# The opening of a three-stage transformer block in one written order, with later loads behind it

## The chip, the cores and the metric

The kernel runs on one core of a Trainium2 chip. The metric is the device time of one execution in microseconds (us). The times of the kernel before are of three runs: 1593.21, 1597.02 and 1598.21 us, median 1597.02 us.

In the profile the engines are PE (TensorE, the matrix products; PEld are its weight loads), DVE (VectorE), ACT (ScalarE), POOL (GpSimd) and SP (SyncE, which here only issues loads). ACT issues some loads too; both engines issue in the order of their own instructions.

## The reference

Two streams of 256 tokens and 1024 features (the latent x and a context) go through two layers. Each layer is a swiglu, a mixer and a second swiglu; the first layer's mixer is a short convolution, the second's is attention. Before each of these stands a normalisation with a modulation whose vectors come from a product with a large matrix:

```
mod  = (silu(c) @ mod_w[i] + mod_b[i])            # 9 vectors of 1024 for the latent
modc = (silu(c_ctx) @ mod_w[i] + mod_b[i])        # and 9 for the context
h    = rms(x, norm_g) * (1 + scale) + shift       # shift, scale: two of the nine
x    = x + 0.5 * gate * ((silu(h @ w13_gate) * (h @ w13_up)) @ w2)
```

The hidden size of a swiglu is 2816, 22 tiles of 128.

## The kernel before

Features lie on the 128 partitions (8 blocks k of 128), tokens on the free axis: 256 latent columns and 256 context columns, 512 together. Every fp32 operand is split into an upper part (`hi`, cast by ACT in `split`, line 98) and a lower part (`lo`, subtracted by DVE, line 99). A product is then three matmuls: upper weights by upper data, upper weights by lower data, lower weights by upper data (`mm3`, lines 122 to 124).

The first swiglu's first three tiles (0, 1, 2) are made in an opening of their own, because their input h needs the modulation's first two vectors (shift `B00`, scale `A00`), which are made on PE, one quarter q (two blocks k) at a time. The opening is a string of steps, `FIRST_STEPS`, taken in order:

- `Pcq` (`mod_pe`): loads a quarter of channel c (1 is scale, 0 is shift; two loads of 512 KB into `pm`), multiplies it by the silu of c on PE (line 757), and copies the row off with ACT.
- `Tcq` (`mod_turn`): turns the row to columns on PE (line 769); DVE adds the bias (line 774).
- `Nq` (`norm_q`): DVE scales x (line 264), ACT adds the shift and casts (`hh`, line 274), DVE subtracts (`hl`, line 275), for two blocks and two streams.
- `F` (`fill`): idle matmuls on a matrix of ones, `FILL` of them.
- `Wi` (`first_w`): loads tile i's weights (1 MB) and splits them.
- `Miq` (`first_mm`): tile i's products for quarter q, 12 matmuls of 512 columns.
- `Hq` (`copy_q`): ACT keeps an fp32 copy of h for the block sums.
- `S` (`load_sc`): loads c for all partitions (`scbc`) and takes its silu.

Only PE keeps this order (`manual_schedule` with PE alone). DVE, ACT and SP are ordered by a scheduler that works from modelled times and lets later work slip in where it thinks an engine is free; a DMA's semaphore is also taken up again only when an earlier load has landed.

After the opening come the gate products of the three tiles (`w13_post`), the block sums of h (`FirstBlocks.sums`: eight sums of 512 columns on DVE, lines 376 to 383, each kept split by ACT and DVE as `th`, `tl`), which serve the block products of later tiles, and six units of modulation (`tick(6)`). A unit (`mod_unit`, line 142) is one DVE reduction of 1024 columns that makes part of a later modulation vector out of a loaded piece of `modT` (1 MB for two or four units) and `scbc`. `tick(n)` adds n to a debt and pays it in whole units. Then `ffn` makes tiles 3 to 7 in the plain way (`tick(5)` after each), projects eight tiles with `w2` (`project`, `tick(ev)` after most of its eight outputs), and goes on with two more thirds of seven tiles and a projection each. `mod_ready` pays at once for what a consumer needs and isn't made yet.

Buffers that matter: three raw weight tiles (`wr`), four split halves (`wh`, `wl`), eight pairs of `gh`, `gl` (which hold tile 2's split weights, the copies H and the gate products in turn), and 16 tiles `hop` (h, the loaded rows, later the block sums).

Of the kernel before, what the change touches and what calls it, by code (L numbers as in the profile page):

```python
# [16 lines left out]
P = 128  # L17
D = 1024
KT = D // P
# [7 lines left out]
KVH = 2  # L27
EPS = 1e-6
WARM = 36
FILL = 8  # L30

FIRST_STEPS = (
    "P10 P00 T10 T00 N0 F W0 M00 W1 P11 P01 T11 T01 N1 H0 M10 W2 M01 P12 H1 M11 P02 T12 T02 "
    "N2 M20 H2 M21 P13 P03 T13 T03 N3 M02 M12 M22 H3 M03 M13 M23 S"
)


# [1 line left out]
def hybrid_kernel(ctx: ExitStack, tc: tile.TileContext, a: dict, out: bass.AP):  # L42
# [53 lines left out]

    def split(hi, lo, src):
        nc.scalar.activation(out=hi, in_=src, func=AF.Copy)  # L98
        nc.vector.tensor_tensor(out=lo, in0=src, in1=hi.bitcast(F32), op=ALU.subtract)  # L99

    def half():

# [515 lines left out]
    def ffn(l, b, h, tot, gate, tail, gs=(), ev=1.5):  # L618
        gs = list(gs)
        i0 = 0  # L620
        for t, n in enumerate(THIRDS):
            between = ()
            if tot == T2:
                heads = []
                if t == 0 and not gs:

                    w = [load_w(a["w13"][l, b, 0])]
                    gs = [new_pair("g") for _ in range(2)]
                    pp = [(psum("pg"), psum("pu")) for _ in range(2)]
                    w13_mm(pp[0], w[0], h, range(KT), 0, S)  # L630
                    flush()
                    w.append(load_w(a["w13"][l, b, 1]))
                    w13_mm(pp[1], w[1], h, range(KT), 0, S)
                    h.sums(0)
                    w13_mm(pp[0], w[0], h, range(KT), S, T2)
                    w13_post(pp[0], gs[0], 0, T2)
                    heads.append(Pair(a["w13"][l, b, 2], h))
                    h.sums(1)
                    heads[0].sums(0)
                    w13_mm(pp[1], w[1], h, range(KT), S, T2)  # L640
                    w13_post(pp[1], gs[1], 0, T2)
                    heads[0].head()
                    h.sums(2)
                    heads[0].sums(1)
                prev = None
                for i in range(len(gs), n):
                    if t == 0 and not heads and i in AS_IS[l, b]:
                        w = load_w(a["w13"][l, b, i])
                        pp = psum("pg"), psum("pu")
                        if prev:  # L650
                            prev.seven()
                        w13_mm(pp, w, h, range(4), 0, T2)
                        if prev:
                            gs.append(new_pair("g"))
                            prev.four(gs[-1])
                            prev = None
                        w13_mm(pp, w, h, range(4, KT), 0, T2)
                        gs.append(new_pair("g"))
                        w13_post(pp, gs[-1], 0, T2)
                        tick(5)  # L660
                        continue
                    if heads:
                        pr = heads.pop(0)
                    else:
                        pr = Pair(a["w13"][l, b, i0 + i], h)
                        pr.sums(0)
                        pr.sums(1)
                        pr.head()
                    pr.five()
                    if prev:  # L670
                        prev.seven()
                    pr.six()
                    if prev:
                        gs.append(new_pair("g"))
                        prev.four(gs[-1])
                    prev = pr

                def last():
                    gs.append(new_pair("g"))
                    prev.four(gs[-1])  # L680

                between = (prev.seven, last) if prev else ()
            else:
                for i in range(n):
                    w = load_w(a["w13"][l, b, i0 + i])
                    gs.append(new_pair("g"))
                    pp = psum("pg"), psum("pu")
                    w13_mm(pp, w, h, range(KT), 0, tot)
                    w13_post(pp, gs[i], 0, tot)
                    tick(1)  # L690
            i0 += n
            box = {}

            def ws2(m):
                if m // 2 not in box:
                    src = a["w2a"][l, b, m // 2] if t == 0 else a["w2b"][l, b, t - 1, m // 2]
                    box[m // 2] = load_raw(src, 2 * n * P)
                raw = box[m // 2]
                o = (m % 2) * n * P
                hi, lo = half()  # L700
                split(hi[:, : n * P], lo[:, : n * P], raw[:, o : o + n * P])
                return lambda k: (hi[:, k * P : k * P + P], lo[:, k * P : k * P + P])

            cur = gs
            end = t == len(THIRDS) - 1
            project(
                ws2, lambda k, c0, c1: (cur[k][0][:, c0:c1], cur[k][1][:, c0:c1]), n,
                gate, tail if end else None, tot, 2 if end and tot == T2 else 0, ev, between,
            )
            gs = []  # L710
# [32 lines left out]

    rows = {}

    def mod_pe(ch, q):


        raws = []
        for i in range(2):  # L750
            raws.append(hot("pm", F32))
            nc.sync.dma_start(raws[i], a["mod0"][ch, q, :, i * 1024 : i * 1024 + 1024])
        pr = psum("pr") if (ch, q) == (1, 0) else psmall("pr")
        for k in range(KT):
            g = 32 * (k % 4)
            o = k % 4 * S
            nc.tensor.matmul(
                pr[g : g + 32, :S], sccol[:, k, :], raws[k // 4][:, o : o + S],
                start=(k < 4), stop=(k >= 4), tile_position=(0, g),
            )  # L760
        row = tp.tile([P, T2], F32, name=nm("row"), tag="gm", bufs=3)
        nc.scalar.copy(row[:, :S], pr[:, :S])
        rows[ch, q] = pr, row
# [14 lines left out]
            op=ALU.add,  # L778
        )

    def norm_q(q):
        k2 = slice(2 * q, 2 * q + 2)
        nc.vector.tensor_tensor(
            out=A00[:, k2, :], in0=A00[:, k2, :], in1=both(normg[:, 0, 0, k2]), op=ALU.mult
        )
        for k in range(2 * q, 2 * q + 2):
            for s in range(2):
                t = None
                if k % 2:
                    t = tp.tile([P, T2], F32, name=nm("t"), tag="sg", bufs=3)[:, :S]  # L790
                ts[k, s] = norm_k(s, k, h, A00, B00, ris[s], t)

    def copy_q(q):
        for s in range(2):
# [10 lines left out]
    def first_mm(i, q):  # L805
        if q == 0:
            pps[i] = psum("pg"), psum("pu")
        w13_mm(pps[i], ws[i], h, range(2 * q, 2 * q + 2), 0, T2)

    ws, gs0 = {}, []  # L810

    def load_sc():
        for v in range(2):
            nc.sync.dma_start(scbc[:, v, :], a["c2"][v : v + 1, :].to_broadcast([P, D]))
            nc.scalar.activation(out=scbc[:, v, :], in_=scbc[:, v, :], func=AF.Silu)

    def first_w(i):
        if i < 2:
            ws[i] = load_w(a["w13"][0, 0, i], fine=True)
            return  # L820
        raw = load_raw(a["w13"][0, 0, i])
        parts = [new_pair("w") for _ in range(4)]
        for j in (0, 2, 1, 3):
            split(*parts[j], raw[:, j * T2 : j * T2 + T2])
        ws[i] = lambda o: tuple(t[:, o % T2 : o % T2 + P] for t in parts[o // T2])

    steps = {
        "P": mod_pe,
# [1 line left out]
        "F": lambda: fill(FILL),  # L830
        "H": copy_q,
        "S": load_sc,
        "W": first_w,
        "N": norm_q,
        "M": first_mm,
    }
    with tc.manual_schedule(engines={mybir.EngineType.PE}):
        fill(WARM)
        sums = [rms_sum(s, (accs[s], accs[s, "last"])) for s in range(2)]
        for step in FIRST_STEPS.split():  # L840
            if step == "P00":
                for s in range(2):
                    ris.append(tp.tile([P, S], F32, name=nm("ris"), tag=f"ris{s}", bufs=1))
                    nc.scalar.copy(ris[s], rms_all(*sums[s]))
            steps[step[0]](*(int(c) for c in step[1:]))
    done[0, 0] = done[0, 1] = 16
    h = FirstBlocks(h, h32)
    for i in range(3):
        gs0.append(new_pair("g"))
        w13_post(pps[i], gs0[i], 0, T2)  # L850
    h.sums()
    tick(6)

    convk = cload("convk", [P, 3, KT])
    qg = cload("qg", [P, 1])
    kg = cload("kg", [P, 1])
    cosT = cload("cosT", [P, S])
    sinT = cload("sinT", [P, S])


    hn = Plain()
    ffn(0, 0, h, T2, lazy_gate(0, 0), tail_norm(0, 1, hn), gs0, 1.8)
    h = hn

    zs = []
# [359 lines left out]
```

## Time and profile before

| what | value |
|---|---|
| median of three runs | 1597.02 us |
| profiled execution | 1595.53 us, its span 1593.7 us |
| mean granted PE clock in the span | 0.993 |
| PE busy | 1568.8 us, 98% |
| DVE busy | 1303.3 us, 82% |
| ACT busy | 721.1 us, 45% |
| moved by DMA | 248.79 MB, mean 156 GB/s |

A line of the timeline is: start, length, engine, line of the code, operation, output, inputs, count, and in brackets how long the engine had been idle and what ended that. A line of a window is: the window, its length, then busy time and count of each engine asked for, the granted PE clock (1.00 is full), the DMA share and GB/s. Matmuls are pipelined and overlap in the records, so the pace is the distance of their starts.

### The profile page before, as it was taken

Reading aid. Unit: us, or ns where it says so; the run is one execution under the profiler, and the core shown is the slowest. Engines: PE = TensorE matmul, PEld = TensorE weight load, DVE = VectorE, ACT = ScalarE, POOL = GpSimd, SP = SyncE. Lnnn points to the kernel's source line nnn. Section 1 sums busy time; section 2 is a strip of 40 time slices with the busy share of each in tenths; the row PEclk is TensorE's granted clock in tenths of the full one; section 3 lists DMA queues with packets and bytes.
Section 4 is the critical chain, followed back from the end, with each engine's and each line's share of the span. In section 5 each row is a group of like instructions: output and inputs, shape, how many; then the busy total and the mean of one; then the engine's idle time right before and its main releaser. Section 6 shows DMA issues by size and latency. Waiting matters only on the chain.

```text
span 1593.7 us, 25820 instructions
## 1 busy us (share of the span) xinstructions
PE 1568.8 (98%) x10666; PEld 1449.7 (91%) x10666; DVE 1303.3 (82%) x1984; ACT 721.1 (45%) x1103; POOL 29.4 (2%) x20
## 2 busy tenths in 40 slices
PE   8999999999999999999999999999999998899999
PEld 7688998999888899989899899899899897899999
DVE  5998888979999879798798879898797789876554
ACT  6522452544322356335345365335255455644443
POOL 0000000000000000000000000000000005200000
PEclk9999999999999999999999999999999999999999
DMA  9465324334565522452342513443433554556452
GB/s 359 181 238 207 110 99 153 133 102 176 177 219 195 175 68 93 148 170 100 129 156 96 180 56 107 158 136 99 169 118 120 208 186 151 200 185 220 166 200 102
DMA packets 39575, 248.79 MB, mean 156 GB/s; under 512 B 5409, under 2 KB 7201, under 8 KB 14625
## 3 DMA queue, kind: packets, MB, share of 16 engines
q1 hardware_dynamic: 36864, 245.38, 43.9%
q10 hardware_dynamic: 2592, 1.76, 0.4%
q8 instruction: 83, 1.36, 0.3%
q14 instruction: 36, 0.29, 0.1%
HBM read 244.77 MB, written 1.05 MB: 154 GB/s over the span
## 4 chain that ended last, share of the span: by engine, by line
PE 92%; DVE 4%; ACT 2%; DMA 1%; issue 0%; POOL 0%; ACTq 0%; DVEq 0%; POOLq 0%
PE py L123 10%; PE py L122 10%; PE py L124 10%; PE p L124 7%; PE p L123 7%; PE p L122 6%; PE q L122 5%; PE q L124 5%; PE q L123 5%; PE pg L122 2%; PE pg L124 2%; PE pg L123 2%; PE pu L124 2%; PE pu L123 2%; PE pu L122 2%; PE pv L122 1%
## 5 line engine op out<-in xcount | busy, mean ns | idle before, releaser
L98 ACT ACTIVATE wh<-wr 128x1024 fp32r<-128x1024 f32 (+2 forms) x276 | 276.4, 1014 | 388.0 <-PE py L123 140.7
L99 DVE TENSOR_TENSOR wl<-wr,wh 128x1024 fp32r<-128x1024 f32 (+2 forms) x276 | 319.9, 1166 | 88.2 <-ACT wh L98 87.9
L142 DVE CUSTOM_DVE_ANT_0 junk<-wr,scbc,modb 128x1024 bf16<-128x1024 f32 x224 | 286.9, 1281 | 31.8 <-DMA wr<-in_modT 29.0
L122 PE MATMUL py<-gh,wh 128*128 128x512 f32 (+1 forms) x746 | 263.3, 353 | 0.0
L123 PE MATMUL py<-gl,wh 128*128 128x512 f32 (+1 forms) x746 | 263.0, 353 | 0.0
L124 PE MATMUL py<-gh,wl 128*128 128x512 f32 (+1 forms) x746 | 262.7, 352 | 0.0
L99 DVE TENSOR_TENSOR wl<-ws,wh 128x1024 fp32r<-128x1024 f32 x108 | 131.6, 1223 | 34.1 <-ACT wh L98 34.0
L124 PEld LDWEIGHTS py<-gh,wl 128*128 128x128 f32 x746 | 141.1, 189 | 19.0
L122 PEld LDWEIGHTS py<-gh,wh 128*128 128x128 f32 x746 | 141.2, 189 | 18.6
L123 PEld LDWEIGHTS py<-gl,wh 128*128 128x128 f32 x746 | 141.2, 189 | 18.1
L98 ACT ACTIVATE wh<-ws 128x1024 fp32r<-128x1024 f32 x108 | 113.9, 1058 | 71.3 <-PE p L123 44.5
L124 PE MATMUL p<-th,wl 128*128 128x256 f32 x432 | 122.3, 283 | 0.0
L123 PE MATMUL p<-tl,wh 128*128 128x256 f32 x432 | 122.2, 283 | 0.0
L122 PE MATMUL p<-th,wh 128*128 128x256 f32 x432 | 122.2, 283 | 0.0
L453 DVE SCALAR_TENSOR_TENSOR x<-py,G,x 128x256 f32<-128x256 f32 x168 | 73.9, 477 | 23.1 <-PE py L124 23.1
L122 PE MATMUL q<-bh,wh 128*128 128x256 f32 x320 | 90.6, 283 | 0.0
L123 PE MATMUL q<-bl,wh 128*128 128x256 f32 x320 | 90.6, 283 | 0.0
L124 PE MATMUL q<-bh,wl 128*128 128x256 f32 x320 | 90.6, 283 | 0.0
L122 PEld LDWEIGHTS p<-th,wh 128*128 128x128 f32 x432 | 82.9, 192 | 0.3
L123 PEld LDWEIGHTS p<-tl,wh 128*128 128x128 f32 x432 | 82.9, 192 | 0.3
L124 PEld LDWEIGHTS p<-th,wl 128*128 128x128 f32 x432 | 82.9, 192 | 0.0
L124 PE MATMUL pg<-hh,wl 128*128 128x256 f32 (+1 forms) x240 | 75.5, 315 | 2.8 <-DVE wl L99 2.7
(236 smaller groups left out, 4045.2 us busy)
## 6 DMA issues: line engine op xcount, KB each, us to landing
wr<-in_w SPq DMA_DIRECT2D x88, 1024.0 KB, 4.9
wr<-in_modT SPq DMA_DIRECT2D x64, 1024.0 KB, 5.0
wr<-in_w2b SPq DMA_DIRECT2D x32, 896.0 KB, 4.6
wr<-in_w2a SPq DMA_DIRECT2D x16, 1024.0 KB, 4.9
pm<-in_mod SPq DMA_DIRECT2D x16, 512.0 KB, 10.0
wr<-in_cw_cx SPq DMA_DIRECT2D x8, 1024.0 KB, 4.9
wr<-in_cw_b SPq DMA_DIRECT2D x4, 1024.0 KB, 5.0
wr<-in_cw_out SPq DMA_DIRECT2D x4, 1024.0 KB, 4.9
```

Of the source, the lines that this page charges most:

```text
L98: nc.scalar.activation(out=hi, in_=src, func=AF.Copy)
L99: nc.vector.tensor_tensor(out=lo, in0=src, in1=hi.bitcast(F32), op=ALU.subtract)
L122: nc.tensor.matmul(ps, wh, mh, start=first, stop=False, **kw)
L123: nc.tensor.matmul(ps, wh, ml, start=False, stop=False, **kw)
L124: nc.tensor.matmul(ps, wl, mh, start=False, stop=last, **kw)
L142: nc.vector.tensor_tensor_reduce(out=junk, in0=raw[:, j * D : j * D + D], in1=scbc[:, v, :], scale=1.0, scalar=modb[:, l, col : col + 1], ...
L453: nc.vector.scalar_tensor_tensor(out=x[:, m, s * S : s * S + S], in0=ps[:, o : o + S], scalar=g[:, m, s : s + 1], in1=x[:, m, s * S : s * ...
```

## The change

The opening's string becomes an order for four queues: PE, DVE, ACT and SP all keep it. For this the steps are cut finer:

- `Lcq` loads the rows that `Pcq` uses, `Ri` a tile's raw weights. `Wip` splits one quarter of them, in the order pair 2, 0, 3, 1.
- `Uq` scales x with A (it needs no shift); `Nqj` adds the shift, casts and subtracts for one block.
- M00 and M10 come ahead of P11 and P01; in them the order of the products changes, and M10 takes those with lower weights last.
- `FILL` is 4 in place of 8.
- `S` stays last, now on ACT and SP too. The five constants of later stages (convk, qg, kg, cosT, sinT) are issued on ACT's queue behind the last silu of `S`.
- The block sums are traced in `ffn` behind tile 3's weight load, and their DVE instructions are put behind the last subtract of tile 1's weights.
- `tick(6)` goes, one unit is taken off the debt ahead of tile 3, and `ev` of the first swiglu goes from 1.8 to 2.1.

```diff
-FILL = 8
+FILL = 4
 FIRST_STEPS = (
-    "P10 P00 T10 T00 N0 F W0 M00 W1 P11 P01 T11 T01 N1 H0 M10 W2 M01 P12 H1 M11 P02 T12 T02 "
-    "N2 M20 H2 M21 P13 P03 T13 T03 N3 M02 M12 M22 H3 M03 M13 M23 S"
+    "L10 L00 R0 R1 P10 T10 U0 P00 L11 L01 T00 F N00 W00 W01 N01 W02 W03 M00 R2 W10 W11 W12 "
+    "W13 H0 M10 P11 L12 P01 L02 T11 U1 T01 N10 N11 M01 W20 W21 H1 M11 W22 W23 P12 L13 P02 L03 "
+    "T12 U2 T02 M20 N20 N21 H2 M21 P13 P03 T13 U3 T03 M02 N30 N31 M12 M22 M03 H3 M13 M23 S"
 )
...
+                        if "T1" not in h.t:
+                            with tc.issue_after(rows["W1"]):
+                                h.sums()
+                            owed[0] -= 1
                         w13_mm(pp, w, h, range(4), 0, T2)
...
+    def mod_load(ch, q):
+        rows[ch, q] = [hot("pm", F32) for _ in range(2)]
+        for i in range(2):
+            nc.sync.dma_start(rows[ch, q][i], a["mod0"][ch, q, :, i * 1024 : i * 1024 + 1024])
...
+    def norm_one(q, j):
+        k = 2 * q + j
+        for s in range(2):
+            hh = pick(h, k, s * S, s * S + S)[0]
+            nc.scalar.activation(
+                out=hh, in_=ts[k, s], func=AF.Identity, bias=B00[:, k, s : s + 1]
+            )
+        for s in range(2):
+            hh, hl = pick(h, k, s * S, s * S + S)
+            nc.vector.scalar_tensor_tensor(
+                out=hl, in0=ts[k, s], scalar=B00[:, k, s : s + 1], in1=hh.bitcast(F32),
+                op0=ALU.add, op1=ALU.subtract,
+            )
...
+        if i < 2 and q == 0:
+            order = [(k, n, lo) for k in range(2) for lo in range(3) for n in range(2)]
+            if i:
+                order.sort(key=lambda o: (o[2] == 2, o[1] if o[2] == 2 else 0))
+            for k, n, lo in order:
+                nc.tensor.matmul(
+                    pps[i][n], ws[i]((1 - n) * 1024 + k * P)[lo == 2],
+                    pick(h, k, 0, T2)[lo == 1], start=k == 0 and lo == 0, stop=False,
+                )
+            return
...
+    def first_w(i, p):
+        j = (2, 0, 3, 1)[p]
+        ins = split(*cut[i][j], raws[i][:, j * T2 : j * T2 + T2])
+        rows[f"W{i}"] = ins.ins
...
-    with tc.manual_schedule(engines={mybir.EngineType.PE}):
+    queues = [nc.tensor, nc.vector, nc.scalar, nc.sync]
+    with tc.manual_schedule(engines={e.engine for e in queues}):
...
-    h.sums()
-    tick(6)
-
-    convk = cload("convk", [P, 3, KT])
...
+    with tc.issue_after(rows["last"]):
+        convk = cload("convk", [P, 3, KT])
+        qg = cload("qg", [P, 1])
...
-    ffn(0, 0, h, T2, lazy_gate(0, 0), tail_norm(0, 1, hn), gs0, 1.8)
+    ffn(0, 0, h, T2, lazy_gate(0, 0), tail_norm(0, 1, hn), gs0, 2.1)
```

More of the change, by code (lines that the diff above doesn't have):

```diff
@@ L98, in split @@
         nc.scalar.activation(out=hi, in_=src, func=AF.Copy)
-        nc.vector.tensor_tensor(out=lo, in0=src, in1=hi.bitcast(F32), op=ALU.subtract)
+        return nc.vector.tensor_tensor(out=lo, in0=src, in1=hi.bitcast(F32), op=ALU.subtract)
     def half():
@@ L744, in hybrid_kernel @@
     rows = {}
+    def mod_load(ch, q):
+        rows[ch, q] = [hot("pm", F32) for _ in range(2)]
+        for i in range(2):
+            nc.sync.dma_start(rows[ch, q][i], a["mod0"][ch, q, :, i * 1024 : i * 1024 + 1024])
     def mod_pe(ch, q):
[L749 to L752, printed above, removed]
+        raws = rows[ch, q]
         pr = psum("pr") if (ch, q) == (1, 0) else psmall("pr")
@@ L779, in mod_turn, with scale_q @@
         )
-    def norm_q(q):
+    def scale_q(q):
         k2 = slice(2 * q, 2 * q + 2)
@@ L790, in norm_q @@
                     t = tp.tile([P, T2], F32, name=nm("t"), tag="sg", bufs=3)[:, :S]
-                ts[k, s] = norm_k(s, k, h, A00, B00, ris[s], t)
+                ts[k, s] = scaled(s, k, A00, ris[s], t)
+    def norm_one(q, j):
[11 more added lines that the diff above has]
+            )
     def copy_q(q):
@@ L807, in first_mm @@
             pps[i] = psum("pg"), psum("pu")
+        if i < 2 and q == 0:
[8 more added lines that the diff above has]
+            return
         w13_mm(pps[i], ws[i], h, range(2 * q, 2 * q + 2), 0, T2)
-    ws, gs0 = {}, []
+    ws, gs0, raws, cut = {}, [], {}, {}
     def load_sc():
@@ L814, in load_sc, with first_raw @@
             nc.sync.dma_start(scbc[:, v, :], a["c2"][v : v + 1, :].to_broadcast([P, D]))
-            nc.scalar.activation(out=scbc[:, v, :], in_=scbc[:, v, :], func=AF.Silu)
-    def first_w(i):
+            last = nc.scalar.activation(out=scbc[:, v, :], in_=scbc[:, v, :], func=AF.Silu)
+        rows["last"] = last.ins
+    def first_raw(i):
+        raws[i] = load_raw(a["w13"][0, 0, i])
         if i < 2:
[L819 to L825, printed above, removed]
+            ts_ = [half() for _ in range(2)]
+            cut[i] = [tuple(t[:, c : c + T2] for t in ts_[j]) for j in range(2) for c in (0, T2)]
+        else:
+            cut[i] = [new_pair("w") for _ in range(4)]
+        ws[i] = lambda o: tuple(t[:, o % T2 : o % T2 + P] for t in cut[i][o // T2])
+    def first_w(i, p):
+        j = (2, 0, 3, 1)[p]
+        ins = split(*cut[i][j], raws[i][:, j * T2 : j * T2 + T2])
+        rows[f"W{i}"] = ins.ins
     steps = {
@@ L832, in hybrid_kernel @@
         "S": load_sc,
+        "L": mod_load,
+        "R": first_raw,
         "W": first_w,
-        "N": norm_q,
+        "U": scale_q,
+        "N": norm_one,
         "M": first_mm,
     }
-    with tc.manual_schedule(engines={mybir.EngineType.PE}):
+    queues = [nc.tensor, nc.vector, nc.scalar, nc.sync]
+    with tc.manual_schedule(engines={e.engine for e in queues}):
         fill(WARM)
@@ L840, in hybrid_kernel @@
         for step in FIRST_STEPS.split():
-            if step == "P00":
+            if step == "U0":
                 for s in range(2):
@@ L850, in hybrid_kernel @@
         w13_post(pps[i], gs0[i], 0, T2)
-    h.sums()
-    tick(6)
-    convk = cload("convk", [P, 3, KT])
[L855 to L858, printed above, removed]
+    with tc.issue_after(rows["last"]):
+        convk = cload("convk", [P, 3, KT])
+        qg = cload("qg", [P, 1])
+        kg = cload("kg", [P, 1])
+        cosT = cload("cosT", [P, S])
+        sinT = cload("sinT", [P, S])
     hn = Plain()
-    ffn(0, 0, h, T2, lazy_gate(0, 0), tail_norm(0, 1, hn), gs0, 1.8)
+    ffn(0, 0, h, T2, lazy_gate(0, 0), tail_norm(0, 1, hn), gs0, 2.1)
     h = hn
```

## The prediction

> **What bounds the kernel now.** I read the page's first table, then a table of windows over the first 128 us, then the chain of waits and the timeline there.
>
> ```profile
> span 1593.7 us, 25820 instructions
> PE 1568.8 (98%) x10666; PEld 1449.7 (91%) x10666; DVE 1303.3 (82%) x1984; ACT 721.1 (45%) x1103; POOL 29.4 (2%) x20
> ```
>
> TensorE (PE) is busy for 98% of the span, so only what shortens PE's time, or removes its waits, can pay. Nothing in the diff takes away a product that the result needs. What PE has to lose therefore lies in the 24.9 us in which it is not busy and in time that is busy but slow or useless. Windows (columns: PE busy and its matmuls, granted clock, DMA share, GB/s):
>
> ```profile
> 0.00:11.60 11.60, 10.57 (x75) 1.00 0.83 287
> 11.60:23.10 11.50, 9.75 (x80) 0.85 0.97 356
> 23.10:31.10 8.00, 6.64 (x54) 1.00 1.01 409
> 31.10:69.40 38.30, 38.07 (x214) 1.00 0.65 254
> 69.40:77.60 8.20, 5.13 (x14) 0.79 0.36 128
> 77.60:128.00 50.40, 50.40 (x224) 1.00 0.66 230
> ```
>
> The last row is the undisturbed pace: 50.40/224 = 0.225 us for a 512-column product, so a block M (12 products: one tile, two k) costs 2.70 us and a whole tile (48) 10.8 us. Up to 31.1 us the DMA share is near 1: the opening is bound by loads. From 31.1 to 69.4 PE works nearly without a hole. The window behind it holds 14 products, worth 3.15 us, in 8.20: 5.05 us are lost just after the first stage. The chain of waits (start, length, what) and the timeline show both places:
>
> ```profile
> 10.67 10.42 DMA cosT<-in_cosT
> 21.09 0.02 issue
> 21.11 8.34 DMA pm<-in_mod
> 29.45 0.04 issue
> 29.49 0.64 PE pr L757 x8
> ...
> 30.68 0.61 PE pr L769 x4
> ```
>
> The last 512 KB of P01's rows is issued only at 21.11 us, when the small cosT load, which is not needed for hundreds of microseconds, has landed. PE gets P01 at 29.49 and the first dependent block at 31.3.
>
> ```profile
> 69.77 0.50 PE L122 MATMUL pg<-hh,wh 128*128 128x512 f32 x1 [0.39 <-ACT wh L98]
> 73.20 0.50 PE L124 MATMUL pg<-hh,wl 128*128 128x512 f32 x1 [2.70 <-DVE wl L99]
> ```
>
> ```profile
> 20.00:21.00 1.00, 1.00 (x6) 0.50 1.03 384
> 75.00:76.00 1.00, 1.00 (x4) 0.50 0.92 385
> ```
>
> Tile 3's products wait 0.39 us for ACT's upper parts of the weights and 2.70 us for DVE's lower parts; then the clock goes to half and products come 4 per us. That is the 5.05: 3.1 of waits, the rest clock.
>
> **The opening, with loads taken away.** Five constants leave the front of ACT's queue; scbc and the modT loads, which before lie between P12 and P13, now follow L03. In the DMA issues (count, KB each, us to landing):
>
> ```profile
> wr<-in_w SPq DMA_DIRECT2D x8, 1024.0 KB, 7.4
> ...
> x<-in_xT SPq DMA_DIRECT2D x4, 512.0 KB, 4.8
> ```
>
> P01 needs the x loads, four row pairs of 1 MB and two weight tiles in front of it: 4 x 0.524 + 8 x 0.524 + 2 x 1.049 = 8.4 MB. By the windows' GB/s, 7.4 MB had moved at 23.1 us and 10.0 MB at 29.45. So early landing is bounded by (8.6 - 7.4)/0.409 = 2.8 us behind 23.1 (8.6 with the small vectors that stay), 25.9, and late by today's 29.45. I take P01 at 27.0, nearer the early end, since the issue that waited for cosT no longer does, while about 1 MB of later loads will still share the engines. The moved loads are hidden: scbc is first read by the modulation's units, which now come later, and convk by the convolution after this swiglu. If SP stalled behind L12 or L13 for a buffer, only L02, L03 and scbc are queued there, and P13 is not wanted before 44 us.
>
> **The opening on PE.** In the old order M10 stands behind P11, P01 and their turns; now M00 and M10 both run ahead of them, in the time in which PE waited for P01. They need one k pair and the first halves of W0 and W1. FILL falls from 8 to 4:
>
> ```profile
> 19.74 3.52 PE L730 MATMUL idle<-ones 128*128 128x128 f32 x16
> ```
>
> That is 3.52 us for 8, up to 23.3, and M00 starts behind it. With 4 it can start 1.8 earlier: I let M00 start at 21.5 and M10 end at 26.9, just before P01 lands. The price of the shift is at M01: no other block hides the way from T01 over the sum on DVE and two casts on ACT to the first product.
>
> ```profile
> 31.76 1.31 ACT L274 ACTIVATE hh<-t,mod 128x256 fp32r<-128x256 f32 x3 [1.14 <-DVE mod L774]
> ```
>
> One cast takes 0.44, the sum and its waits about 0.5: 1.4 with the subtract. P01's start to the end of T01 is today 29.49 to 31.29, 1.8. So M01 starts at 27.0 + 1.8 + 1.4 = 30.2, taken as 30.4 for the second subtract. Ten blocks remain where at 31.1 there were eleven: 27.0 us. The row products and turns between them stay in PE's order:
>
> ```profile
> 37.11 1.07 PE L757 MATMUL pr<-pm,sccol 128*32 128x256 f32 x16
> ...
> 41.07 1.07 PE L757 MATMUL pr<-pm,sccol 128*32 128x256 f32 x16
> 42.07 1.22 PE L769 MATMUL pr<-rowsum,row 128*128 128x2 f32 x8
> ...
> 48.80 1.93 PE L757 MATMUL pr<-pm,sccol 128*32 128x256 f32 x32
> 50.66 1.22 PE L769 MATMUL pr<-rowsum,row 128*128 128x2 f32 x8
> ```
>
> They make 6.5 us. Eleven blocks and these are 36.2 of the 38.3; the other 2.1 are waits, partly because DVE did units of the modulation first:
>
> ```profile
> 57.04 0.16 DVE L774 TENSOR_TENSOR A<-pr,sb 128x4 f32<-128x4 f32 x1
> ```
>
> The fourth pair's sum runs at 57.04 although its turn was over at 51.9. The written order puts U3 and N3 there at once, and the units behind. I keep 0.5 of the 2.1 (bounds 0 and 2.1). The stage then ends at 30.4 + 27.0 + 6.5 + 0.5 = 64.4 instead of 69.4: **5.0 us**.
>
> What the written order queues: behind each row copy that waits on ACT lie W2's splits and the copies H, wanted one block later; behind U and N on DVE lies the same. W2 is first needed by M20, after M01, M11 and two row products. In M10 the products with lower parts come last, so W1's subtracts have eight products (1.8 us) of cover. I cost these at nothing.
>
> **Behind the stage.** Today the block sums wait for H3, which waits for the late fourth pair, and their casts and subtracts lie ahead of tile 3's weights on ACT and DVE. Now H3 can run near 50 us. W0's buffers come free with M03, two blocks before the stage ends; in those 5.4 us ACT needs two casts of 1024 columns and DVE two subtracts of 1.22, plus one gate product. So I take back 4.5 of the 5.05 and leave 0.5 for queueing; bounds 0 and 5.05. The clock goes with the wait: a 2.70 us hole was enough to halve it. The Trainium skill, "TensorE: Matmul & The Clock Gate", section "Why this matters for your kernels", asks for no idle gaps over about 3 us; by that this gap would cost no clock and the gain here would be 2.6 instead of 4.5, in sum 1589.4. The row at 75 us shows the half clock after a shorter gap, so the trace disagrees, and I keep its number.
>
> **DVE's balance.** Groups on DVE from 60 to 128 us, and its busy time by windows:
>
> ```profile
> L142 DVE CUSTOM_DVE_ANT_0 junk<-wr,scbc,modb 128x1024 bf16<-128x1024 f32 x27 | 34.6, 1282 | 2.0 <-DMA wr<-in_modT 1.5
> L99 DVE TENSOR_TENSOR wl<-wr,wh 128x1024 fp32r<-128x1024 f32 x12 | 14.4, 1219 | 0.5 <-ACT wh L98 0.5
> L99 DVE TENSOR_TENSOR tl<-hr,th 128x512 fp32r<-128x512 f32 x8 | 5.1, 685 | 0.0
> ```
>
> ```profile
> 60.00:128.00 68.00, 63.95 (x96) 0.97 0.57 200
> 128.00:172.00 44.00, 40.51 (x63) 1.00 0.51 182
> 240.00:285.00 45.00, 37.73 (x59) 1.00 0.45 158
> 340.00:400.00 60.00, 51.17 (x94) 1.00 0.43 154
> ```
>
> Six units of tick(6) and one of the owed count leave the front; 22 ticks in the three projections go from 1.8 to 2.1, 6.6 units more. That moves 7 units of 1.28, 9.0 us, from the stage to the windows at 128, 240 and 340 us, 3.0 each, where DVE has 3.5, 7.3 and 8.8 us free. I take 0 (bounds 0 and 9.0). In tiles 3 to 7 (54 us) DVE has 24 units, 30.8 us; eleven weight subtracts, 13.4; and seven gate products with their subtracts at about 0.685, 9.6: 53.8 together. It just fits, if the block sums (eight sums, eight subtracts, 11.0 us) are done before. The first stage without units has the room: its own DVE work is nearly all 256- and 512-column operations.
>
> **The sum.** 5.0 + 4.5 = 9.5 us. The profiled execution took 1595.53 us (span 1593.7), so 1586.0 for it; it lies 1.5 below the median of 1597.02 us, and against that I predict 1587.5. About 0.3% (4.8 us) is what a measurement of this kernel tells from no change: the line is at 1592.2.
>
> **Rivals.**
> A, the wait returns: tile 3 still waits for DVE, because the scheduler places sums or gate products ahead of its subtracts. Only 5.0 remains: 1592.0, on the line. For it: DVE is 94% busy behind 60 us. Against: two blocks of cover. 0.14, of which 0.08 counts as faster.
> B, given back: the moved units are exposed in the projections, 9.0 us: 1596.5. For it the 3.5 us free at 128; against the other two windows. 0.08.
> C, slower: DVE becomes the bound through the whole first swiglu. If the block sums lie behind the stage, 11.0 us are over in tiles 3 to 7; with DVE then behind at the first projection nothing absorbs the 9.0 of moved units. -5.0 - 5.05 + 11.0 + 9.0 = +10: 1607. It decides if the last block sum ends after tile 3 (about 75 us). Against: they need only H3. 0.08.
> D, the change does less in the opening: other loads still slip in and P01 lands near 29.4, or M00 runs at half clock (the row at 20 us shows that state) and needs 2.4 more. M01 starts at about 32.8 instead of 30.4: gain 2.6 + 4.5, 1589.9. 0.10. [...]
> The forecast itself: 0.60.
>
> **Numbers.** Faster by over 0.3%: 0.60 + 0.10 + 0.08 = 0.78; within: 0.06 + 0.08 = 0.14; slower: 0.08. The low end takes P01 at 25.9 (-1.1), no waits (-1.0) and three us for the runs' own spread (1593.21 to 1598.21 us): 1582.5. The high end takes in D and A with 2 us of spread: 1594.0; B and C, 0.16, stay outside.
>
> **What would show it.** Right: no cosT in the chain before 60 us; M10 ahead of P01's products; P01 near 27; M23's end near 64; no wait over 1 us and no half clock between 60 and 80; the first unit on DVE after 50 us, the last block sum before 64. Wrong: a wait of PE on DVE's lower parts between 64 and 130, or new ones in the projections at 125 to 165 or 235 to 280 us.

## The result and the profile after

| | before | after |
|---|---|---|
| median of 20 runs each, us | 1596.58 | 1591.39 |
| lowest to highest, us | 1592.36 to 1598.21 | 1589.64 to 1596.1 |
| ratio, 95% interval | | 0.9971 [0.9965, 0.9978] |
| profiled execution, us (span) | 1595.53 (1593.7) | 1592.14 (1590.3) |

The changed kernel is faster by 5.2 us. Forecast was 1587.5, a gain of 9.5. So the sign is right, the result lies in the range, and little more than half of the expected gain came. In a second set of runs the same kernel stood at 1592.91 us against 1595.11, ratio 0.9985 [0.9973, 0.9997]. The gain is real and small: 0.29% in the first set and 0.15% in the second, so that only the first is about as large as the 0.3% that the forecast asked of a faster kernel.

The totals of the profile after:

```profile
span 1590.3 us, 25784 instructions
PE 1566.4 (98%) x10658; PEld 1450.2 (91%) x10658; DVE 1304.4 (82%) x1984; ACT 719.5 (45%) x1103; POOL 29.5 (2%) x20
```

PE is still the bound. The table of windows over the start, with the same cuts as before (PE busy and its matmuls, granted clock, DMA share, GB/s):

```profile
11.60:23.10 11.50, 9.61 (x82) 1.00 1.02 413
...
31.10:69.40 38.30, 37.08 (x207) 0.96 0.55 206
69.40:77.60 8.20, 8.20 (x38) 1.00 0.32 119
```

Two things are to be seen. Between 69.4 and 77.6 us there are 38 products where there were 14, and no hole: the loss behind the first stage is gone, and the profile names no wait of PE from 60 to 130 us. The first stage itself, the second row, got worse in one respect: its clock is 0.96 where it was 1.00, and it has 1.22 us of idle where it had 0.23. The timeline of PE shows where (start, length, what, idle before it and who ended it):

```profile
20.43 0.50 PE L836 MATMUL pg<-hh,wh 128*128 128x512 f32 x1 [0.78 <-ACT wh L100]
...
26.02 0.62 PE L836 MATMUL pu<-hh,wl 128*128 128x512 f32 x2
26.57 1.93 PE L765 MATMUL pr<-pm,sccol 128*32 128x256 f32 x32
28.44 1.22 PE L777 MATMUL pr<-rowsum,row 128*128 128x2 f32 x8
32.28 0.50 PE L124 MATMUL pg<-hh,wh 128*128 128x512 f32 x1 [2.62 <-ACT hh L805]
...
34.02 0.63 PE L125 MATMUL pu<-hl,wh 128*128 128x512 f32 x1
34.44 0.63 PE L126 MATMUL pu<-hh,wl 128*128 128x512 f32 x1
...
37.70 0.39 PE L124 MATMUL pu<-hh,wh 128*128 128x512 f32 x1
```

L836 is M00 and M10, the next two are P11 with P01 and their turns, and L124 begins M01. Nothing waits for P01's rows any more, but M01 waits 2.62 us for the casts of h, and then products start every 0.43 us for a while, and later every 0.225. The granted clock by stretches of 2 us says why:

```profile
30.00:32.00 2.00, 0.00 (x0) 1.00 1.06 426
32.00:34.00 2.00, 1.70 (x4) 0.78 1.03 412
34.00:36.00 2.00, 2.00 (x6) 0.50 0.98 397
36.00:38.00 2.00, 2.00 (x9) 0.87 1.04 406
```

What M01 waited for stands on DVE's timeline:

```profile
29.15 0.16 DVE L782 TENSOR_TENSOR A<-pr,sb 128x4 f32<-128x4 f32 x1 [2.00 <-PE pr L777]
29.35 0.16 DVE L791 TENSOR_TENSOR A<-A,normg 128x4 f32<-128x4 f32 x1
29.55 1.67 DVE L266 SCALAR_TENSOR_TENSOR t<-x,A,ris 128x256 f32<-128x256 f32 x4
31.14 0.15 DVE L782 TENSOR_TENSOR mod<-pr,modb 128x4 f32<-128x4 f32 x1
```

The third row is U1, the four scalings of x (two blocks, two streams): 1.67 us between T11's sum and T01's sum, which the casts on ACT need.

One number for each part of the run: the first start of the first projection's products (`py`) and of the convolution's (`pc`), from the views of these two tiles. Before, they start at 128.9 and 392.1 us; after, at 122.2 and 387.7. So 6.7 us are gained up to the first projection, and 2.3 of them are lost again ahead of the convolution. They are lost near 278 us, where the chain of block products begins in the last third:

```profile
277.26 0.28 PE L126 MATMUL q<-hh,wl 128*128 128x256 f32 x1
278.31 0.38 PE L124 MATMUL q<-th,wh 128*128 128x256 f32 x1 [0.77 <-ACT wh L100]
...
279.57 0.38 PE L126 MATMUL q<-th,wl 128*128 128x256 f32 x1 [0.52 <-DVE wl L101]
```

Against their usual pace of 0.12 us these products lost 1.8 us there. Before has no wait of PE at all between `py` and `pc`. The 2.3 us are of this one execution; the second profile of the same kernel lost 1.4 between the two points, with a single wait of 0.5 us.

### The profile page after: what moved, and what is told of

It is laid out like the page before. It is cut to its first block, busy times and chain, and to the rows that moved or that the text cites. A ratio compares the mean times of both kernels' runs of the same rounds, so it can differ in the third digit from the quotient of the medians.

```text
span 1590.3 us, 25784 instructions
## 1 busy us (share of the span) xinstructions
PE 1566.4 (98%) x10658; PEld 1450.2 (91%) x10658; DVE 1304.4 (82%) x1984; ACT 719.5 (45%) x1103; POOL 29.5 (2%) x20
## 4 chain that ended last, share of the span: by engine, by line
PE 92%; DVE 4%; ACT 2%; DMA 1%; issue 1%; POOL 0%; ACTq 0%; DVEq 0%; POOLq 0%
PE py L124 9%; PE py L125 9%; PE py L126 9%; PE p L126 6%; PE p L125 6%; PE p L124 6%; PE q L126 5%; PE q L124 5%; PE q L125 5%; PE pg L124 3%; PE pg L125 3%; PE pg L126 3%; PE pu L126 3%; PE pu L125 3%; PE pu L124 3%; PE pv L124 1%
## 5 line engine op out<-in xcount | busy, mean ns | idle before, releaser
L124 PE MATMUL py<-gh,wh 128*128 128x512 f32 (+1 forms) x746 | 263.3, 353 | 0.0
L124 PEld LDWEIGHTS py<-gh,wh 128*128 128x128 f32 x746 | 141.2, 189 | 18.4
L126 PE MATMUL p<-th,wl 128*128 128x256 f32 x432 | 122.2, 283 | 0.0
L125 PE MATMUL p<-tl,wh 128*128 128x256 f32 x432 | 122.2, 283 | 0.0
L124 PE MATMUL p<-th,wh 128*128 128x256 f32 x432 | 122.2, 283 | 0.0
L124 PE MATMUL q<-bh,wh 128*128 128x256 f32 x320 | 90.7, 283 | 0.0
L124 PEld LDWEIGHTS p<-th,wh 128*128 128x128 f32 x432 | 82.9, 192 | 0.3
L124 PE MATMUL pg<-hh,wh 128*128 128x256 f32 (+1 forms) x236 | 74.3, 315 | 3.7 <-ACT hh L805 2.6
```

The source lines that it names most:

```text
L124: nc.tensor.matmul(ps, wh, mh, start=first, stop=False, **kw)
L125: nc.tensor.matmul(ps, wh, ml, start=False, stop=False, **kw)
L126: nc.tensor.matmul(ps, wl, mh, start=False, stop=last, **kw)
```

## The experiments

Times in this table are medians; a ratio goes to the runs of the kernel before beside it, on the same chip, so ratios compare and times less so. The last three columns are from the one profiled execution of each.

| kernel | us | ratio [95%] | py, us | pc, us | between |
|---|---|---|---|---|---|
| after, units back | 1602.36 | 1.0041 [1.0027, 1.0055] | 133.8 | 397.0 | 263.2 |
| after, M10 late | 1588.27 | 0.9951 [0.9935, 0.9967] | 119.5 | 384.2 | 264.7 |
| after, U1 late | 1590.66 | 0.9971 [0.9957, 0.9985] | 125.4 | 390.1 | 264.7 |
| after, hole filled | 1589.54 | 0.9955 [0.9937, 0.9973] | 121.2 | 386.0 | 264.8 |
| after, constants at the front | 1593.24 | 0.9980 [0.9969, 0.9992] | 125.3 | 390.0 | 264.7 |
| before, units moved | 1593.00 | 0.9981 [0.9968, 0.9993] | 125.7 | 390.9 | 265.2 |
| before, constants moved | 1594.44 | 0.9984 [0.9969, 0.9998] | 126.2 | 389.4 | 263.2 |
| before, both moved | 1593.90 | 0.9980 [0.9972, 0.9989] | 124.1 | 389.2 | 265.1 |
| M10 late, ticks of 1.8 | 1587.26 | 0.9950 [0.9931, 0.9970] | 119.4 | 382.6 | 263.2 |
| the same, FILL 8 | 1590.61 | 0.9965 [0.9953, 0.9978] | 121.5 | 384.8 | 263.3 |
| after, again | 1592.91 | 0.9985 [0.9973, 0.9997] | 122.7 | 387.3 | 264.6 |
| M10 late, ticks of 1.8, again | 1587.87 | 0.9954 [0.9940, 0.9969] | 120.6 | 383.9 | 263.3 |

### M10 behind T01

```diff
-    "W13 H0 M10 P11 L12 P01 L02 T11 U1 T01 N10 N11 M01 W20 ...
+    "W13 H0 P11 L12 P01 L02 T11 U1 T01 M10 N10 N11 M01 W20 ...
```

> The changed kernel with M10 moved on PE from ahead of P11 to behind T01. Theory: the 2.62 us wait ahead of M01 is the way from T01 over DVE and ACT that no block hides, and the half clock behind it is its consequence; with M10 (2.7 us) there, the wait and the slow products (about 1.8 us) go, P01 must have landed by about 26.5 us, and the first product of the first projection starts 3 to 4.4 us earlier than 122.2 us. Rival: P01's landing binds, so PE waits for it instead of working on M10, and the start moves by less than 1 us.

Its timeline of PE:

```profile
25.45 0.64 PE L765 MATMUL pr<-pm,sccol 128*32 128x256 f32 x8 [0.17 <-PE pr L765]
26.61 0.64 PE L765 MATMUL pr<-pm,sccol 128*32 128x256 f32 x8 [0.52 <-DMA pm<-in_mod]
27.23 1.17 PE L777 MATMUL pr<-rowsum,row 128*128 128x2 f32 x8
28.26 0.49 PE L836 MATMUL pg<-hh,wh 128*128 128x512 f32 x1
...
31.12 0.46 PE L124 MATMUL pg<-hh,wh 128*128 128x512 f32 x1
```

PE now meets P01's last rows as they land (0.52 us of wait), M10 (L836) fills the way over DVE and ACT, and M01 starts at 31.12 without a wait and at full clock. That is 1.16 us earlier than in after. M01 to `py` takes 88.4 us against 89.9, and the two make the 2.7 us by which `py` is earlier. The forecast was 3 to 4.4 us. Behind T01 is also where M10 stood in the kernel before, so this run takes back one step of the change. That step's place thus decides the size of the gain in the opening.

### U1 behind T01

```diff
-    "W13 H0 M10 P11 L12 P01 L02 T11 U1 T01 N10 N11 M01 W20 ...
+    "W13 H0 M10 P11 L12 P01 L02 T11 T01 U1 N10 N11 M01 W20 ...
```

> The changed kernel with U1 (A times g and four scalings on DVE) written behind T01's sum instead of ahead of it. Theory: the second sum stood 1.5 us behind the four scalings on DVE; it now runs near 29.7 us, the first cast near 30.3, M01 about 1 us earlier than 32.28, and the shorter hole may keep the clock; the first projection starts 1 to 2.9 us earlier than 122.2 us. Rival: the way is bound by the scalings themselves, the order does not matter, 0.

Timeline of PE:

```profile
34.98 0.50 PE L124 MATMUL pg<-hh,wh 128*128 128x512 f32 x1 [1.85 <-ACT hh L805]
36.02 0.79 PE L125 MATMUL pg<-hl,wh 128*128 128x512 f32 x1 [0.54 <-DVE hl L810]
36.61 0.63 PE L126 MATMUL pg<-hh,wl 128*128 128x512 f32 x1
```

The wait is 1.85 + 0.54 = 2.39 us instead of 2.62, and the clock is halved all the same. The sum's place behind the scalings therefore made only 0.2 us of the wait: the casts need the scalings as well as the sum, and with the sum first the subtracts still stand behind all four scalings. The theory forecast M01 1 us earlier; its rival, that the order doesn't matter, came. A finer order on DVE, with the casts and subtracts of one block ahead of the scalings of the next, was not tried; what covered the wait in these runs is work on PE. The `py` of this execution is no measure of the edit, since it ran M00 at half clock as well, from 15 to 25 us.

### Idle products in the hole

```diff
-    "... T11 U1 T01 N10 N11 M01 W20 ...
+    "... T11 U1 T01 N10 N11 G M01 W20 ...
...
+        "G": lambda: fill(2 * FILL),
```

> The changed kernel with eight idle products (about 2.2 us) added on PE between T01 and M01, nothing else. Theory: the half clock from 32.8 to 36.4 us comes from the hole ahead of M01; with it filled M01 still starts near 32.3 us, its products run at full clock, and the first projection starts 1.5 to 2 us earlier than 122.2 us although work was added. Rival: the clock falls for the waits before (P11 to T01) or for some other reason, and the start stays or moves later.

Timeline of PE, then its clock by stretches:

```profile
30.04 2.03 PE L736 MATMUL idle<-ones 128*128 128x128 f32 x16
32.80 0.50 PE L124 MATMUL pg<-hh,wh 128*128 128x512 f32 x1 [0.73 <-ACT hh L805]
```

```profile
34.00:36.00 2.00, 2.00 (x11) 1.00 0.98 377
```

Eleven matmuls in the stretch in which after had six at 0.50. M01 to `py` takes 88.4 us, the same as with M10 late: the half clock behind a 2.62 us hole costs 1.5 us, and 2 us of work that computes nothing earns it back. Here the clock is told apart from the wait, which stays. `py` came 1.0 us earlier and not the 1.5 to 2 of the forecast, because M01 itself starts 0.5 later. It is one execution, but the others agree. All five profiles of the written order with a hole ahead of M01 (after twice, U1 late, units back, constants at the front) show 0.50 on M01's products. Of the five without a hole of that length, four hold 1.00 from 27 to 40 us; the fifth, with `FILL` 8, fell to 0.50 at 29.7 behind a wait of 1.1.

### The units back in the opening

```diff
                         if "T1" not in h.t:
                             with tc.issue_after(rows["W1"]):
                                 h.sums()
-                            owed[0] -= 1
...
         w13_post(pps[i], gs0[i], 0, T2)
+    tick(6)
...
-    ffn(0, 0, h, T2, lazy_gate(0, 0), tail_norm(0, 1, hn), gs0, 2.1)
+    ffn(0, 0, h, T2, lazy_gate(0, 0), tail_norm(0, 1, hn), gs0, 1.8)
```

> The changed kernel with the units of the modulation as before: tick(6) ahead of the first swiglu, no unit taken off the debt, 1.8 instead of 2.1. Theory: the written order and not the moved units removed the 5.05 us behind the opening, so tile 3 waits at most 1 us; the two waits near 278 us (1.3 us) and what comes with them (2.2 us between the first projection and the convolution) go. Rival: the moved units removed it, and a wait of 3 us with half clock comes back at about 68 us.

It is slower than before, where the forecast had tile 3 wait at most 1 us. The waits of PE from 60 to 130 us (in total, times, longest):

```profile
PE pg L124 <- ACT wh L100: 3.7, 1, 3.7
PE pu L126 <- DVE wl L101: 1.9, 1, 1.9
PE pg L126 <- DVE wl L101: 0.6, 1, 0.6
```

The one of 1.9 ends at 73.55 us, at tile 3, where the prediction had expected the written order to take it away. DVE's timeline there:

```profile
61.67 1.29 DVE L144 CUSTOM_DVE_ANT_0 junk<-wr,scbc,modb 128x1024 bf16<-128x1024 f32 x1 [0.23 <-ACT scbc L847]
...
69.87 1.28 DVE L144 CUSTOM_DVE_ANT_0 junk<-wr,scbc,modb 128x1024 bf16<-128x1024 f32 x1
...
72.28 1.22 DVE L101 TENSOR_TENSOR wl<-wr,wh 128x1024 fp32r<-128x1024 f32 x1
```

Units start when scbc is ready, and in the written order its silu stands last on ACT; before ran units from 46.4 us, between the sums. So six of them here lie between 61.7 and 71.1, ahead of tile 3's lower parts. DVE doesn't catch up inside the swiglu, and at 109.7 comes the 3.7 us wait and another half clock (windows give 0.66 from 110 to 115). This is the prediction's rival C in small, and it shows that the units' move isn't a side effect to be costed at nothing: without it the written order loses 8.9 us (M01 to `py` 98.8 against 89.9). The 2.3 us between `py` and `pc` are gone, though: 263.2, as in before.

### One part alone, on the kernel before

Units moved, nothing else:

```diff
-    tick(6)
+    owed[0] -= 1
...
-    ffn(0, 0, h, T2, lazy_gate(0, 0), tail_norm(0, 1, hn), gs0, 1.8)
+    ffn(0, 0, h, T2, lazy_gate(0, 0), tail_norm(0, 1, hn), gs0, 2.1)
```

> The kernel before with only the units of the modulation moved: tick(6) gone, one unit off the debt, 2.1 instead of 1.8; the opening stays ordered on PE alone. New theory, after the run with the units put back: the 5.05 us behind the opening are lost because units stand on DVE ahead of the fourth quarter, the block sums and tile 3's weights, whoever writes the order. Then the wait of 2.7 us and the half clock near 74 us go here too and the first product of the first projection starts at 122.5 to 125 us instead of 128.9. Rival: the written order is what removed it, and the start stays within 1 us of 128.9.

```profile
70.02 0.50 PE L124 MATMUL pg<-hh,wl 128*128 128x512 f32 x1 [1.81 <-DVE wl L99]
```

PE's timeline has one wait behind the stage, 1.81 us, for 0.39 and 2.70 before. `py` gains 3.2 us and 2.0 of them are given back by `pc`. The result lies between the theory (`py` at 122.5 to 125, no wait) and its rival (128.9).

Constants moved, nothing else (issued behind the last silu, with `rows["last"]` as in the change):

```diff
-    convk = cload("convk", [P, 3, KT])
...
-    sinT = cload("sinT", [P, S])
+    with tc.issue_after(rows["last"]):
+        convk = cload("convk", [P, 3, KT])
...
+        sinT = cload("sinT", [P, S])
```

> The kernel before with only the five constants moved behind the last silu on ACT's queue. Theory of the prediction: the last load of P01's rows no longer waits for cosT, P01 lands 2 to 3 us earlier than 29.49, and the rest of the opening moves with it: the first projection starts 1.5 to 3 us earlier than 128.9 us. Rival: DMA bandwidth sets P01's landing, and it moves by less than 1 us.

```profile
25.56 1.93 PE L757 MATMUL pr<-pm,sccol 128*32 128x256 f32 x32
...
50.59 0.64 PE L757 MATMUL pr<-pm,sccol 128*32 128x256 f32 x8 [2.92 <-DMA pm<-in_mod]
```

P11 and P01 run at 25.56 us without a wait, where P01 stood at 29.49. But the fourth pair's rows are now late, by 2.92 us, and the clock is halved behind it. The chain of waits shows what they stood behind:

```profile
42.34 3.55 DMA convk<-in_convk
...
45.95 4.59 DMA pm<-in_mod
```

It is one of the moved constants again. In the old order the last silu is over at 41.0 us and the last of these rows are issued at 46, so the constants have only changed the load that they hold up. `py` gains 2.7, and PE has no wait behind the stage, although the units stand where they were.

Both of these together:

> The kernel before with the constants behind the silu and the units moved, the opening still ordered on PE alone. Theory: these two parts make the gain and the order written for four queues adds little; the first projection starts near 123 us (the changed kernel: 122.2) and the ratio to before is 0.9965 to 0.9975. Rival: the written order is needed to use them; the start stays at 125 to 126 us, as with either part alone, and the ratio at 0.998 or above.

```profile
PE pr L757 <- DMA pm<-in_mod: 3.0, 1, 3.0
PE pg L122 <- ACT wh L98: 1.5, 1, 1.5
```

These are all its waits of PE from 20 to 130 us. The wait for the fourth pair's rows stays (its chain has convk in front of it too), and the two gains don't add: `py` 4.8 us early, not 5.9. In after, where all rows are issued by 29.8 us and the constants only from 53.2 on, that wait isn't there.

This run also says what the written order is worth by itself. Its ratio, 0.9980 [0.9972, 0.9989], can't be told from that of the change as it was made, 0.9971 and 0.9985; at `py` the change is 1.4 to 1.9 us ahead. The theory had forecast 0.9965 to 0.9975, and `py` near 123.

### Constants back at the front

```diff
-    with tc.issue_after(rows["last"]):
-        convk = cload("convk", [P, 3, KT])
...
+    convk = cload("convk", [P, 3, KT])
...
```

(the five loads as in before, the rest as in after)

> The changed kernel with the five constants loaded at the front again. Theory: P01 lands up to 3 us later than the 26.6 us at which PE takes it without a wait now, M01 moves back by as much, and the first projection starts 1 to 3 us later than 122.2 us. Rival: M10 covers the later landing or the loads slip in at no cost, below 1 us.

```profile
28.95 1.93 PE L765 MATMUL pr<-pm,sccol 128*32 128x256 f32 x32
30.82 1.22 PE L777 MATMUL pr<-rowsum,row 128*128 128x2 f32 x8
34.66 0.79 PE L124 MATMUL pg<-hh,wh 128*128 128x512 f32 x1 [2.62 <-ACT hh L805]
```

PE reaches P11 2.4 us later than in after, and M01 keeps its 2.62. PE doesn't wait for P01's rows here: M00 starts 0.95 us later, at 21.38, since its weights come later, and the rest is the clock, which was halved from 23 to 26.4 us. So not all of the 3.1 us at `py` belong to the loads.

### The best order with smaller ticks

M10 late as above, and

```diff
-    ffn(0, 0, h, T2, lazy_gate(0, 0), tail_norm(0, 1, hn), gs0, 2.1)
+    ffn(0, 0, h, T2, lazy_gate(0, 0), tail_norm(0, 1, hn), gs0, 1.8)
```

> The changed kernel with M10 behind T01 and with 1.8 units per projection step instead of 2.1 (no tick(6), so 7 units go to later stages). Theory: the wait of the block products near 275 us comes from units that hold the weight buffers and DVE in the second projection; with fewer of them the 2.3 us between the first projection and the convolution go, and the whole is 1.5 to 2.5 us faster than with M10 behind T01 alone. Rival: the units left over are paid in the last projection or in the convolution, where DVE is nearly full, and the time stays or grows.

From `py` to `pc` 263.2 us again, with no wait near 278: the windows from 270 to 280 us hold 8.71 us of work in after and

```profile
270.00:280.00 10.00, 10.00 (x78) 1.00 0.54 179
```

here. The units go elsewhere, not away (224 in both); 88 instead of 84 of them now run behind 700 us. `pc` is 1.6 us earlier than with M10 late alone. In the whole time this doesn't show, though 1.5 to 2.5 us were forecast: the two ratios are 0.9950 and 0.9951.

The same kernel with `FILL = 8`:

> The changed kernel with M10 behind T01, 1.8 units per step, and FILL 8 again. Theory: M00 starts up to 0.4 us later and PE waits for P01's load anyway, so nothing changes in the median (within 1 us of the 1587.3 us with FILL 4) and the first projection starts at 119.4 us. Rival: the shorter fill leaves M00 at half clock in some executions (seen in three profiles of the experiments near 24 us), so FILL 8 narrows the spread and makes the median 1 to 2 us faster.

`py` came at 121.5, 2.1 us later, but this execution had the half clock at 16 to 19 and at 30 to 33 us, and the intervals overlap (0.9965 against 0.9950). The rival, 1 to 2 us faster with the longer fill, didn't come. What the shorter fill is worth stays open.

Since single executions differ by a few us in the opening, after and the best kernel ran once more, on one chip:

> The changed kernel as it is, beside the next one on the same chip. Its ratio to before should come again near 0.997. In its profile M01 should again wait about 2.6 us; where a half clock falls in the opening may differ between executions.

> The changed kernel with M10 behind T01 and 1.8 units per projection step, beside the one before on the same chip. If the hole ahead of M01 and the units in the second projection are what the change left on the table, it is 3 to 5 us faster than the changed kernel here too; rival: the earlier ratio of 0.9950 was a lucky draw of five runs, and it lies within 1.5 us of the changed kernel.

1592.91 and 1587.87 us, with intervals that don't meet (0.9985 [0.9973, 0.9997] and 0.9954 [0.9940, 0.9969]). The better order is worth 5.0 us over the change as it was made, and some 7 to 9 over before. After showed its hole of 2.62 us and the half clock behind it again (0.50 from 34 to 37 us), though not the ratio near 0.997 that was forecast. What made the best kernel better is the place of M10: the smaller ticks alone don't show in the whole time.

## Why the prediction was right, and where it wasn't

**What bounds it: right.** Loads set the opening, and PE the rest; the loss behind the first stage was there to be had.

**P01 and the loads: right.** Predicted 27.0, bounds 25.9 and 29.45. PE took P11 and P01 at 26.57 without a wait, and with M10 late the last rows are waited for until 26.61. Constants back at the front: 28.95, in part for the clock. M00 was put at 21.5 and started at 20.43; M10's end, put at 26.9, came at 26.6. (The early bound was 1.2/0.409 = 2.9 us and not 2.8 behind 23.1, so 26.0.)

**M01: the step that failed.** Predicted 30.4, measured 32.28. "P01's start to the end of T01 is today 29.49 to 31.29, 1.8" took over a duration from an order in which P11 had run earlier. In the new one P11's products and turns stand behind M10 too, so it is 26.57 to 29.66, 3.1. And "1.4 with the subtract" for the way from T01 to M01 left out U1's four scalings, 1.67 us on DVE, and one of two casts: it is 2.62. So -0.43 for the earlier P01, +1.3, and +1.0 for 2.62 against 1.6: together the 1.9 us. Every instruction of the moved step had to be counted, and the scalings are a step of their own in the new order.

**The half clock in the opening: left out.** From M01 to the stage's end the prediction had 34.0 us (27.0 + 6.5 + 0.5); it took 32.28 to 67.83, 35.55. The 1.55 more is the half clock behind the hole, which the filled hole measured at 1.5. The 0.5 kept for waits was about right, but the 2.1 it was taken from were misread: the row says 38.07 us busy of 38.30, so only 0.23 was idle, and the rest lies in products that started more than 0.225 us apart (two of them 0.5 and 0.6, near 60 and 62 us). The prediction knew that 2.70 us had been enough to halve the clock behind the stage, and costed none at M01 because it believed the hole to be 1.4. The rule of no gaps over about 3 us, in the Trainium skill, "TensorE: Matmul & The Clock Gate", section "Why this matters for your kernels", would have let 2.62 pass; these runs don't.

So the stage ends at 67.83 instead of 64.4, and the term of 5.0 us measured 1.6 (69.4 - 67.8). This is nearer to the size of rival D than to the forecast, but by another mechanism: P01 was not late, nor M00 slow. That the whole still fell into the range is owed to its width.

**Behind the stage: right size, wrong reason.** 4.5 was taken of 5.05, and all of it came: 6.7 at `py` less 1.6. The reason given was that the written order lets H3 run early (near 50 us; it ran at 54.8) and gives tile 3's weights two blocks of cover. With the units back in, the written order waits there again; with the units moved alone, the old order still waits 1.81. Yet no part is needed as such, since two kernels in the old order have no wait there either. What decides is which comes first, tile 3 on PE or the end of its second subtract on DVE:

| kernel | tile 3 starts on PE, us | its second subtract ends, us | waits of PE |
|---|---|---|---|
| before | 69.8 | 73.1 | 0.39 + 2.70 |
| before, units moved | 67.6 | 69.9 | 1.81 |
| before, constants moved | 71.8 | 71.4 | none |
| before, both moved | 69.7 | 69.3 | none |
| after | 67.8 | 68.2 | none |

With the constants moved PE itself is late, having lost its time at the fourth pair's rows. After alone has both an early PE and an early DVE, and there the written order and the moved units work together; that the size came out right was luck. In after the units started at 58.90, tile 3's two subtracts stand at 65.3 and 67.0, and the subtracts of the block sums were put behind them (68.2 to 74.9). The eight sums themselves were over by 58.7, so "the last block sum before 64" held for the sums and not for their subtracts, and nobody waited for those.

**The units at nothing: a miss of 2.3 us,** inside the bounds of 0 to 9.0 (1.4 to 2.0 in the other profiles with ticks of 2.1). It is rival B in part, in the window from 240 to 285 us for which 7.3 us of free time had been counted. DVE has that time on average, but five units stand close together between 263.6 and 270.8 us, ahead of the lower parts that PE waits for. With ticks of 1.8 the loss is gone in every kernel that had them (263.2 or 263.3 between `py` and `pc`); whether the units did it through ACT or through DVE, the two that PE waited for, was not followed.

Together 1.6 + 5.05 - 2.3 = 4.4 us, which is what the trace has at `pc` (392.1 - 387.7). The spans differ by 3.4, the medians by 5.2; the rest of the span, from `pc` on, varies between 1199.8 and 1204.8 us in the fourteen profiles.

Rival A didn't come in after, and did in the kernel with the units back; rival C didn't come either, but that kernel shows its start. The condition "It decides if the last block sum ends after tile 3" was badly put: what decided was what stood ahead of tile 3's subtracts, not when the sums ended.

## What to carry to other kernels

When an order is written out by hand, go through every way that leaves PE and comes back (a small product, a sum, scalings, a cast, the next product), and put a whole block of products behind each; a block placed in front of such a way instead, here to fill a wait for a load, moved the hole behind it. Take the length of that way from its instructions on all queues in the new order, not from a distance in the old one. Filler work that is moved off a stage has to be counted where it arrives, in short stretches and not as free time of a long window.

## What was not expected of the hardware

A hole of 2.62 us on PE was enough for a granted clock of 0.50 from some 0.8 us after the work had come back until 36.5 us, about 3.4 us, and it cost 1.5 us; with 2.03 us of idle products in it, the clock stayed at 1.00. The single hole of 1.81 us with the units moved had the half clock behind it too (0.64 from 70 to 72 us, 0.51 from 72 to 74). In the openings of seven of the fourteen profiles the clock also fell to 0.50 between 14 and 27 us, where the other seven, some with nearly the same instructions, ran at 1.00 throughout. This may explain part of the runs' scatter of several us; its trigger wasn't found.

Five small loads, 128 KB at most, set when a 512 KB load could be issued. In before the four loads of the second pair went out over 5.34 us from 16.09 on, after over 3.03 us from 9.70 on. SP's own waits name them. In before it stands still for the landings of four of the five (below); in after for none of them; with the constants back at the front for the four again (4.0, 2.6, 0.9 and 0.8 us); with only the constants moved, 4.1 us for convk.

```profile
SPq L94 <- DMA qg<-in_qg: 4.6, 1, 4.6
SPq L814 <- DMA sinT<-in_sinT: 2.0, 1, 2.0
SPq L752 <- DMA cosT<-in_cosT: 2.0, 1, 2.0
SPq L752 <- DMA kg<-in_kg: 1.4, 1, 1.4
```

So it is the issue on SP that waited until a small load had landed. Why cosT, with its 128 KB, took 10.42 us to land was not followed.
